# Routed experts on one core: only used rows gathered, results scattered in two column halves, fixed buffers, another general path

## The chip, the cores and the metric

The kernel runs on one core of one Trainium2 chip. What counts is the device time of one execution in microseconds; the median of several runs is given. PE is the matrix engine, PEld its weight loads, DVE, ACT and POOL the vector, scalar and general engines, SP the engine that starts most DMAs.

## The reference, cut to what matters

One layer over 512 tokens of width 1024 in float32: an RMS norm and one wide projection, three attention branches (gated linear attention in chunks, attention over selected keys, attention over a memory of 256 rows), gated output projections, a residual, and then experts in groups:

```
g_sel    = argmax(h @ w_r1 + b_r1)                      # 4 groups
e_prob   = softmax(the 4 logits of that group in h @ w_r2 + b_r2)
top_p, top_i = top_k(e_prob, 2), normed; weight = g_prob * top_p
hid      = silu(h @ w_gate[e]) * (h @ w_up[e]) * weight  # 16 experts, 1024 -> 256
x        = x + sum over e of hid[e] @ w_down[e]          # 256 -> 1024
```

Each token goes to 2 of 16 experts. The kernel returns x, 512 x 1024.

## The kernel before

Products of float32 are made of three passes each (high x high, high x low, low x high): ACT casts a weight tile to its high part (line 94), DVE forms the rest (line 95), PE runs the three products (lines 102 to 104 for the experts). All stages up to the second residual are as in the change and aren't told here. `out_gemm` (line 1016) forms the residual x, POOL multiplies it by the norm's gain (line 1054) and writes it to `h2d` in DRAM (line 1055), ACT's queue writes x itself to `out`. The router (`route`, `place`) finds each token's two experts and its place among an expert's tokens.

An expert has C = 96 slots. `rows` (line 1212) forms `idx0`: for each slot of each expert the token's row. A slot without a token gets a row number from 512 up, and for these `h2d` and `out` have 96 rows more, which a tile of zeros fills (lines 953 to 958).

The loop over the 16 experts (line 1342) runs an order given by letters, `ORDER = "0H12at3bh"`. In round e, "0", "1", "2", "3" are the gate and up products of expert e in four parts (`up`, line 1288; a piece of part 3 takes the raw weight, line 1300), "H" transposes the hidden values of expert e-1, "a" and "b" are the two column halves of its down product (`down`, line 1321), each copied by ACT into half of y (line 1328), "t" transposes the gathered tokens of expert e+1 (`tokens_t`, line 1268), "h" forms the hidden values of e. After "b" the whole y, 96 x 1024, is added to `out` by one indirect DMA of POOL (`scatter`, line 1331). At the start of round e POOL also gathers the tokens of expert e+2 (`gather`, line 1258), and SP fetches the twelve weight tiles of expert e+4 (`fetch`, lines 839 and 844). Expert 0's tokens aren't gathered but placed by products (line 1149).

The gathered tile xg and the result y are taken from one ring of four buffers (`tag="wr"`, `WR = 4`), in the order in which the scheduler reaches them. POOL's DMAs are counted by eight counters, DMASW0 to 7, which they take in turn; SP's and ACT's by DMAHW0 to 7. Each engine runs its instructions in the order laid down at build time.

At the end the largest expert's count is loaded into a register of each engine (line 1378), and a general path runs if it is over 96 (`tc.If`, line 1379): further blocks of 96 slots with gathers and scatters of their own.

```
    got, xt, hid, ht, ys = {}, {}, {}, {}, {}
    got[1] = gather(idx0[:, 1:2])
...
        if e + 2 < ne:
            got[e + 2] = gather(idx0[:, e + 2:e + 3])
...
                    ys[o] = wp.tile([C, D], F32, tag="wr", name="y", bufs=WR)
                else:
                    down(ys[o], *ht[o], wts[o], int(op in "bd"))
                if op in "bd":
                    scatter(ys[o], idx0[:, o:o + 1])
```

Of the kernel before, what the change touches and what calls it, by code (L numbers as in the profile page):

```python
# [18 lines left out]
P = 128  # L19
# [28 lines left out]
def hybrid(ctx, tc, a, out):  # L48
# [904 lines left out]
    zrow = slot([P, 512], F32, "zrow")  # L953
    G.memset(zrow, 0.0)
# [95 lines left out]
    def residual(t, c, ps, x, ss):  # L1050
# [12 lines left out]
        nc.scalar.dma_start(out[t * P:(t + 1) * P, c * 512:(c + 1) * 512], x)  # L1063
# [125 lines left out]
    ne = 16  # L1189

    def mark(c, t0):
# [3 lines left out]
        if c:  # L1195
            p4 = small.tile([P, 4], F32, name="p4")
            V.tensor_scalar(p4, pos[:, tt, :].rearrange("p t c -> p (t c)"), float(-c * C), None, op0=OP.add)
        V.tensor_tensor(out=oh, in0=slots[:, None, :].to_broadcast([P, 4, C]), in1=p4.to_broadcast([P, 4, C]),
                        op=OP.is_equal)
        V.tensor_scalar(vals[:, tt, :, 2], pos[:, tt, :], -1.0, float(c * C - 1), op0=OP.mult, op1=OP.add)  # L1200
        return oh
# [10 lines left out]
    def rows(c, idx):  # L1212
        """c: the chunk of slots; None for the first one, whose marks are kept in ohs0."""
        pi = ap_.tile([C, 16 * 3], F32, tag="lg", name="lg")
        ohs = ohs0 if c is None else []
        for t0, k in ((0, L0), (2, -1)):
            with ExitStack() as held:
                if c is None and k is not None:
                    held.enter_context(tc.issue_after(late[k].ins))
                ohs.append(mark(c or 0, t0))  # L1220
                spread(pi, ohs, 0, 3, t0, False)
# [3 lines left out]
        found = V.tensor_scalar(idx, fi, float(T - 1), None, op0=OP.add)  # L1225
        return found if c is None else ohs
# [9 lines left out]
    # the array stays busy while the last tokens are routed  # L1236
# [12 lines left out]
    found = rows(None, idx0)  # L1249
# [12 lines left out]
    def tokens_t(xg, placed=None):  # L1262
        xH, xL = [], []
        for c in range(2):
            if placed is None:
                tp = ap_.tile([P, 4, C], F32, tag="tp", name="tp")
                for k in range(4):
                    PE.transpose(tp[:, k, :], xg[:, :, 4 * c + k], ident[0:C, 0:C])
            else:
                tp = placed[c]  # L1270
            h = sp.tile([P, 4, C], F32R, tag="x", name="xgh", bufs=4)
            l = sp.tile([P, 4, C], F32R, tag="x", name="xgl", bufs=4)
            raw = sp.tile([P, C], F32, tag="xr", name="xgr", bufs=2) if c else None
            n = 4 - c
            if placed is None:
                split_into(h[:, 0:n, :], l[:, 0:n, :], tp[:, 0:n, :])
            else:
                for k in (0, 2):
                    m = min(k + 2, n)
                    split_into(h[:, k:m, :], l[:, k:m, :], tp[:, k:m, :])  # L1280
# [24 lines left out]
    def hidden(ps, cwt):  # L1305
        hid = half([C, P, 2], F32, "hid")
# [5 lines left out]
    def hidden_t(hid):  # L1312
        tp = ap_.tile([P, 2, C], F32, tag="tp", name="tp")
        for k in range(2):
            PE.transpose(tp[:, k, :], hid[:, :, k], ident[0:C, 0:C])
        hh = half([P, 2, C], F32R, "hh")
        hl = half([P, 2, C], F32R, "hl")
# [3 lines left out]
    def down(y, hh, hl, ws, c):  # L1321
        wh = wp.tile([P, 2, 512], F32R, tag="wh", name="wh", bufs=WH)
        wl = wp.tile([P, 2, 512], F32R, tag="wl", name="wl", bufs=WH)
        ps = gp.tile([C, 512], F32, tag="g", name="g")
# [9 lines left out]
    got, xt, hid, ht, ys = {}, {}, {}, {}, {}  # L1334
    got[1] = gather(idx0[:, 1:2])
# [6 lines left out]
    for e in range(ne):  # L1342
        if e + NF < ne:
            fetch(e + NF, after=found if e == E0 else None)
        if e + 2 < ne:
            got[e + 2] = gather(idx0[:, e + 2:e + 3])
        for op in ORDER if e < ne - 1 else LAST:
# [31 lines left out]
    with tc.If(cval > C):  # L1379
        more = []  # L1380
        for c in range(1, -(-T // C)):
            idx = const.tile([C, ne], I32, name=f"idx{c}")
            cwt = const.tile([C, ne, 2], F32, name=f"cwt{c}")
            ohs = rows(c, idx)
            weights(ohs, cwt)
            more.append((idx, cwt))
        with tc.For_i(0, ne, 1) as e:
            one = bass.ds(e, 1)
            ws = load_expert(*[a[n][one].rearrange("o r c -> (o r) c") for n in ("w_gate", "w_up", "w_down")])
            for idx, cwt in more:  # L1390
                ix = small.tile([C, 1], I32, name="ix")
                V.tensor_copy(ix, idx[:, one])
                cw = small.tile([C, 2], F32, name="cwx")
                V.tensor_copy(cw, cwt[:, one, :].rearrange("p o q -> p (o q)"))
                xH, xL = tokens_t(gather(ix))
                ps = gp.tile([C, 512], F32, tag="g", name="g")
                for kc in range(4):
                    up(ps, xH, xL, ws, kc)
                hh, hl = hidden_t(hidden(ps, cw))
                y = wp.tile([C, D], F32, tag="wr", name="y", bufs=WR)  # L1400
                for i in range(2):
                    down(y, hh, hl, ws, i)
                scatter(y, ix)
# [25 lines left out]
```

## Time and profile before

| | |
|---|---|
| median of 3 runs | 1003.43 us (1003.26 to 1009.3) |
| span of the profiled execution, first to last instruction | 1002.3 us |
| PE busy, share of the span | 943.1 us, 94% |
| DVE, ACT, POOL busy | 639.2, 473.3, 133.0 us |
| DMA | 138.71 MB, 138 GB/s over the span |
| expert loop, first transposes to the last copy into y | 813.4 to 983.8 us |

The page gives one execution; the median of the runs is 1.1 us above its span. Busy shares are means over stages that are bound by different things, so the loop is read stretch by stretch below.

### The profile page before, as it was taken

To read this page: it belongs to the slowest core of one execution; us is meant where nothing else is said; L and a number is where in the kernel's file an instruction comes from. 1 tells how busy PE (TensorE), PEld (TensorE's weight loads), DVE (VectorE), ACT (ScalarE), POOL (GpSimd) and SP (SyncE) were. 2 spreads that over 40 slices of the span, in tenths; PEclk is the share of its full clock that TensorE was granted. 3 is DMA by queue.
4 is the path that set the end of the run, shared out by engine and by line. 5 is a ranking of instruction groups with operands and counts; after the bars stand their busy time and mean duration, and the time that the engine had idled before them with its cause. 6 is when DMAs were issued, how large, how long until landed. Compare 5 with 4: busy or idle time off the path is not lost. (4 is left out here: it accounts for less than half of the span.)

```text
span 1002.3 us, 13004 instructions
## 1 busy us (share of the span) xinstructions
PE 943.1 (94%) x4425; PEld 754.6 (75%) x4425; DVE 639.2 (64%) x1581; ACT 473.3 (47%) x946; POOL 133.0 (13%) x120
## 2 busy tenths in 40 slices
PE   7999999999999969999999999999999889988992
PEld 5778776887888858887888888878888767756661
DVE  6895668779876545467544633662554678867861
ACT  5675443454222524466333323443234258867771
POOL 4002123001320131000000000001011212222221
PEclk9999999999999989999999999999999799999997
DMA  7755221222233212221332222247575379999972
GB/s 230 224 142 158 85 64 43 65 62 83 86 106 90 82 43 66 82 64 43 89 100 85 85 84 85 64 126 252 169 252 177 128 227 324 299 308 313 305 202 46
DMA packets 73529, 138.71 MB, mean 138 GB/s; under 512 B 8930, under 2 KB 11568, under 8 KB 73456
## 3 DMA queue, kind: packets, MB, share of 16 engines
q1 hardware_dynamic: 66656, 119.56, 38.8%
q0 software_dynamic: 5616, 16.14, 7.0%
q10 hardware_dynamic: 1184, 2.11, 0.6%
q8 instruction: 37, 0.61, 0.2%
q14 instruction: 36, 0.29, 0.1%
HBM read 125.59 MB, written 11.27 MB: 137 GB/s over the span
## 5 line engine op out<-in xcount | busy, mean ns | idle before, releaser
L94 ACT CAST wh<-wr 128x1024 fp32r<-128x1024 f32 (+1 forms) x124 | 127.6, 1030 | 263.9 <-PE g L145 154.9
L95 DVE TENSOR_TENSOR wl<-wr,wh 128x1024 fp32r<-128x1024 f32 (+1 forms) x124 | 150.1, 1211 | 151.1 <-ACT wh L94 145.1
L140 PE MATMUL g<-hh,wh 128*128 128x512 f32 (+1 forms) x424 | 169.9, 401 | 0.4 <-DVE mvl L98 0.4
L145 PE MATMUL g<-hl,wh 128*128 128x512 f32 (+1 forms) x424 | 166.7, 393 | 0.0
L146 PE MATMUL g<-hh,wl 128*128 128x512 f32 (+1 forms) x424 | 165.9, 392 | 0.0
L95 DVE TENSOR_TENSOR wl<-mw,wh 128x512 fp32r<-128x512 f32 (+1 forms) x188 | 112.6, 641 | 9.5 <-ACT wh L94 9.4
L94 ACT CAST wh<-mw 128x512 fp32r<-128x512 f32 (+1 forms) x188 | 101.1, 587 | 11.3 <-PE g L104 10.6
L140 PEld LDWEIGHTS g<-hh,wh 128*128 128x128 f32 x424 | 80.8, 191 | 17.8 <-issue 1.9
L146 PEld LDWEIGHTS g<-hh,wl 128*128 128x128 f32 x424 | 80.7, 190 | 16.0
L145 PEld LDWEIGHTS g<-hl,wh 128*128 128x128 f32 x424 | 80.7, 190 | 14.8 <-issue 0.2
L140 PE MATMUL g<-wh,hh 128*128 128x512 f32 x160 | 63.3, 395 | 0.0
L145 PE MATMUL g<-wl,hh 128*128 128x512 f32 x160 | 63.1, 394 | 0.0
L146 PE MATMUL g<-wh,hl 128*128 128x512 f32 x160 | 62.7, 392 | 0.0
L102 PE MATMUL g<-wh,xgh 128*96 128x512 f32 x108 | 48.2, 446 | 0.5 <-ACT wh L94 0.5
L437 POOL PARTITION_ALL_REDUCE dqsq<-dqsq x8 | 26.7, 3359 | 135.2 <-ACT dqsq L429 77.5
L103 PE MATMUL g<-wl,xgh 128*96 128x512 f32 x108 | 43.6, 403 | 0.5 <-DVE wl L95 0.3
L104 PE MATMUL g<-wh,xgl 128*96 128x512 f32 x108 | 43.6, 404 | 0.0
L606 ACT ACTIVATE dp<-dp,nm,rs_y 128x128 f32<-128x128 f32 (+3 forms) x32 | 20.9, 654 | 35.4 <-DVE nm L605 35.3
L964 POOL MEMSET tmp<- 128x128 f32 x1 | 0.2, 205 | 267.6 <-PE tp L795 267.6
L145 PEld LDWEIGHTS g<-wl,hh 128*128 128x128 f32 x160 | 30.2, 189 | 6.2 <-issue 0.5
L140 PEld LDWEIGHTS g<-wh,hh 128*128 128x128 f32 x160 | 30.1, 188 | 6.4 <-issue 0.5
L146 PEld LDWEIGHTS g<-wh,hl 128*128 128x128 f32 x160 | 30.1, 188 | 6.0
(425 smaller groups left out, 2015.7 us busy)
## 6 DMA issues: line engine op xcount, KB each, us to landing
wr<-in_w_in_dram SPq DMA_DIRECT2D x72, 512.0 KB, 3.6
mw<-in_w_gate_dram SPq DMA_DIRECT2D x64, 256.0 KB, 8.1
mw<-in_w_up_dram SPq DMA_DIRECT2D x64, 256.0 KB, 8.2
mw<-in_w_down_dram SPq DMA_DIRECT2D x64, 256.0 KB, 7.8
wr<-in_w_mem_kv_dram SPq DMA_DIRECT2D x16, 512.0 KB, 5.5
wr<-in_w_o_mem_dram SPq DMA_DIRECT2D x8, 512.0 KB, 3.9
wr<-in_w_o_dsa_dram SPq DMA_DIRECT2D x8, 512.0 KB, 3.9
wr<-in_w_o_gla_dram SPq DMA_DIRECT2D x8, 512.0 KB, 3.8
```

The costliest lines, as they stand in the source:

```text
L94: hi = A.copy(h, src)
L95: lo = V.tensor_sub(l, src, h.bitcast(F32))
L102: PE.matmul(ps, sh, mh, start=first, stop=False)
L103: PE.matmul(ps, sh, ml, start=False, stop=False)
L104: PE.matmul(ps, sl, mh, start=False, stop=last)
L140: i = PE.matmul(ps, sh, mh, start=first, stop=False)
L145: PE.matmul(ps, sh, ml, start=False, stop=False)
L146: i = PE.matmul(ps, sl, mh, start=False, stop=last)
L437: G.partition_all_reduce(flat, flat, P, bass_isa.ReduceOp.add)
L606: A.activation(p, p, AF.Exp, bias=nm[:, t:t + 1], scale=rs, accum_out=sm[:, t:t + 1])
L964: G.memset(tmp, 1.0)
```

## The change

The 96 rows of padding in `h2d` and `out` go. Gathers and scatters get a bound: a slot whose row number is over 511 is skipped (`bounds_check=T - 1, oob_is_err=False`). The gathers write into two fixed buffers, cleared once by POOL, so that a skipped slot holds old but finite values; their weights are zero. `out` becomes two tensors, one for each half of the columns. Each half of y is scattered by itself as soon as it is copied, from two fixed buffers in turn. The general path treats all 512 tokens for each expert, with plain DMAs of SP in place of POOL's gathers and scatters. On these inputs the largest expert has 83 tokens, so it isn't entered.

```
-    h2d = tc.dram_tile([T + C, D], F32, name="h2d")
-    for c in range(2):
-        nc.gpsimd.dma_start(h2d[T:T + C, c * 512:(c + 1) * 512], zrow[0:C, :])
-        nc.gpsimd.dma_start(out[T:T + C, c * 512:(c + 1) * 512], zrow[0:C, :])
+    h2d = tc.dram_tile([T, D], F32, name="h2d")
...
-    def gather(idx):
-        xg = wp.tile([C, P, KB], F32, tag="wr", name="xg", bufs=WR)
-        nc.gpsimd.indirect_dma_start(out=xg.rearrange("p i k -> p (i k)"), out_offset=None, in_=h2d[:, :],
-                                     in_offset=bass.IndirectOffsetOnAxis(ap=idx, axis=0))
-        return xg
+    xb = [wp.tile([C, P, KB], F32, tag="wr", name="xg", bufs=WR) for _ in range(2)]
+    yb = [wp.tile([C, 2, 512], F32, tag="wr", name="y", bufs=WR) for _ in range(2)]
+    for x in xb:
+        G.memset(x, 0.0)
+
+    def gather(e):
+
+        nc.gpsimd.indirect_dma_start(out=xb[e % 2].rearrange("p i k -> p (i k)"), out_offset=None, in_=h2d[:, :],
+                                     in_offset=bass.IndirectOffsetOnAxis(ap=idx0[:, e:e + 1], axis=0),
+                                     bounds_check=T - 1, oob_is_err=False)
+        return xb[e % 2]
...
-        A.copy(y[:, c * 512:(c + 1) * 512], ps)
-
-    def scatter(y, idx):
-        nc.gpsimd.indirect_dma_start(out=out, out_offset=bass.IndirectOffsetOnAxis(ap=idx, axis=0),
-                                     in_=y, in_offset=None, compute_op=OP.add)
+        return ps
+
+    def scatter(e, c, ps):
+        y = yb[e % 2][:, c, :]
+        A.copy(y, ps)
+        nc.gpsimd.indirect_dma_start(out=out[c], in_=y, in_offset=None, compute_op=OP.add,
+                                     out_offset=bass.IndirectOffsetOnAxis(ap=idx0[:, e:e + 1], axis=0),
+                                     bounds_check=T - 1, oob_is_err=False)
...
-                    ys[o] = wp.tile([C, D], F32, tag="wr", name="y", bufs=WR)
                 else:
-                    down(ys[o], *ht[o], wts[o], int(op in "bd"))
-                if op in "bd":
-                    scatter(ys[o], idx0[:, o:o + 1])
+                    c = int(op in "bd")
+                    scatter(o, c, down(*ht[o], wts[o], c))
...
             for t in range(NT):
...
+                nc.sync.dma_start(xg.rearrange("p i k -> p (i k)"), h2d[rs, :])
...
+                    nc.sync.dma_start(o, out[c][rs, :])
+                    V.tensor_add(o, o, down(hh, hl, ws, c, P))
+                    nc.sync.dma_start(out[c][rs, :], o)
```

POOL's order in the expert loop, before, from the scatter of expert 0's result on. A row has the line, the tensors (the number tells tiles of one name apart) and what the row waits for:

```order
L1331 DMA out_0_dram<-y_7415,idx0_7150 608x1024 [waits DMAHW5_49,DMAHW3_49,DMAHW6_49,DMAHW1_49,Activation_49]
L1258 DMA xg_7661<-h2d_6440,idx0_7150 96x1024 [waits DMASW3_49]
L1331 DMA out_0_dram<-y_7549,idx0_7150 608x1024 [waits Activation_49]
L1258 DMA xg_7795<-h2d_6440,idx0_7150 96x1024 [waits DMASW5_49,DMASW0_49,PE_49]
L1331 DMA out_0_dram<-y_7683,idx0_7150 608x1024 [waits Activation_49]
L1258 DMA xg_7929<-h2d_6440,idx0_7150 96x1024 [waits DMASW7_49,DMASW1_49,PE_49]
L1331 DMA out_0_dram<-y_7817,idx0_7150 608x1024 [waits Activation_49]
```

And in the changed kernel, from the first half of expert 1's result on:

```order
L1328 DMA out_0_dram<-y_7184,idx0_7144 512x512 [waits DMASW6_49,Activation_49]
L1252 DMA xg_7182<-h2d_6438,idx0_7144 96x1024 [waits DMASW5_49,PE_49]
L1328 DMA out_1_dram<-y_7184,idx0_7144 512x512 [waits DMASW0_49,Activation_49]
L1328 DMA out_0_dram<-y_7183,idx0_7144 512x512 [waits DMASW1_49,Activation_49]
L1252 DMA xg_7181<-h2d_6438,idx0_7144 96x1024 [waits DMASW7_49,PE_49]
L1328 DMA out_1_dram<-y_7183,idx0_7144 512x512 [waits DMASW3_49,Activation_49]
L1328 DMA out_0_dram<-y_7184,idx0_7144 512x512 [waits DMASW4_49,Activation_49]
L1252 DMA xg_7182<-h2d_6438,idx0_7144 96x1024 [waits DMASW2_49,PE_49]
L1328 DMA out_1_dram<-y_7184,idx0_7144 512x512 [waits DMASW6_49,Activation_49]
```

Before, a gather waits for the counter of the scatter in the row above it (the scatters take DMASW3, 5, 7, 1 here), for that of an older gather and for PE, and each scatter for ACT alone. Now a gather waits for the older gather in its buffer and for PE; each half waits for ACT and for the same half of the expert before.

POOL's order around the end of the If, before:

```order
L1387 REGISTER_ALU
L1387 COMPARE_AND_BRANCH
L1387 UNCONDITIONAL_BRANCH [waits DMASW5_49,DMASW4_49,DMASW6_49,DMASW3_49,DMASW7_49,DMASW2_49,DMAHW0_49,DMASW1_49,DMAHW1_49,DMASW0_49,DMAHW2_49,SP_sequencer_49,DMAHW3_49,DVE_sequencer_49,DMAHW4_49,PE_sequencer_49,DMAHW5_49,Activation_se
L1379 ISA [waits DMASW4_49,DMASW5_49,DMASW3_49,DMASW6_49,DMASW2_49,DMASW7_49,DMASW1_49,DMASW0_49]
L1379 UNCONDITIONAL_BRANCH
L1425 ISA [waits barrier_Pool_Activation_PE_DVE_SP_gather]
```

And now:

```order
L1388 REGISTER_ALU
L1388 COMPARE_AND_BRANCH
L1388 UNCONDITIONAL_BRANCH [waits DMASW5_49,DMASW4_49,DMASW6_49,DMASW3_49,DMASW7_49,DMASW2_49,DMAHW0_49,DMASW1_49,DMAHW1_49,DMASW0_49,DMAHW2_49,SP_sequencer_49,DMAHW3_49,DVE_sequencer_49,DMAHW4_49,PE_sequencer_49,DMAHW5_49,Activation_se
L1375 UNCONDITIONAL_BRANCH
L1428 ISA [waits barrier_Pool_Activation_PE_DVE_SP_gather]
```

The ISA row of line 1379, which waits for all eight counters of POOL's DMAs, is gone.

POOL's order where the residual is multiplied, before the loop, first the four zero writes and then the multiplies, before:

```order
L964 MEMSET tmp_6447 128x128 [waits PE_49]
L965 AFFINE_SELECT tmp_6447<-tmp_6447 128x128 [waits Pool_49]
L954 MEMSET zrow_6436 128x512 [waits PE_49]
L957 DMA h2d_6440<-zrow_6436 96x512 [waits DMASW3_49,Pool_49]
L958 DMA out_0_dram<-zrow_6436 96x512
L957 DMA h2d_6440<-zrow_6436 96x512
L958 DMA out_0_dram<-zrow_6436 96x512
L1054 TENSOR_TENSOR xg_6622<-xr_6509,gffn_6420 128x512 [waits DMAHW6_49,DVE_49,Activation_49]
L1055 DMA h2d_6440<-xg_6622 128x512 [waits Pool_49]
```

And now, with the two clears of the fixed buffers:

```order
L1049 TENSOR_TENSOR xg_6616<-xr_6503,gffn_6420 128x512 [waits DMAHW6_49,DVE_49,Activation_49]
L1050 DMA h2d_6438<-xg_6616 128x512 [waits DMASW3_49,Pool_49]
L1248 MEMSET xg_7181 96x1024 [waits DMAHW4_49,DMAHW2_49,DMAHW7_49,DMAHW0_49,Activation_49]
L1049 TENSOR_TENSOR xg_6641<-xr_6505,gffn_6420 128x512 [waits DVE_49]
L1050 DMA h2d_6438<-xg_6641 128x512 [waits Pool_49]
L1049 TENSOR_TENSOR xg_6672<-xr_6507,gffn_6420 128x512 [waits DVE_49]
L1050 DMA h2d_6438<-xg_6672 128x512 [waits Pool_49]
L1049 TENSOR_TENSOR xg_6703<-xr_6509,gffn_6420 128x512 [waits DVE_49]
L1050 DMA h2d_6438<-xg_6703 128x512 [waits Pool_49]
L1248 MEMSET xg_7182 96x1024 [waits DMAHW5_49,DMAHW3_49,DMAHW7_49,DMAHW1_49,DVE_49]
L1049 TENSOR_TENSOR xg_6846<-xr_6727,gffn_6422 128x512 [waits DMAHW7_49,DVE_49,PE_49]
L1049 TENSOR_TENSOR xg_6877<-xr_6729,gffn_6422 128x512 [waits DVE_49,PE_49]
```

The zero writes are gone, and the clears stand after the first and after the fourth multiply. On the other engines the rows up to the If, and their order, are the same as before.

## Rows read from the trace of the kernel before

**Rows 1.** Busy time of each engine in three stretches: the stretch, its length, then busy us (instructions) of PE, PEld, DVE, ACT, POOL, the mean granted PE clock as a share of full speed, the mean busy share of the 16 DMA engines, GB/s.

```profile
813.40:880.00 66.60, 66.60 (x323) 49.12 (x324) 57.17 (x109) 56.08 (x127) 13.34 (x10) 0.97 1.02 311
880.00:966.00 86.00, 75.73 (x345) 54.15 (x344) 62.57 (x116) 61.68 (x135) 17.86 (x14) 0.94 1.04 310
966.00:983.80 17.80, 15.73 (x69) 10.06 (x67) 11.88 (x24) 13.37 (x29) 4.46 (x3) 1.00 0.44 66
```

**Rows 2.** PE's timeline: start, us, engine, line, operation, in brackets the idle time before it and what ended it. L1268 are the transposes of the gathered tokens, L1300 the products with the raw weight.

```profile
813.40 1.25 PE L1268 MATMUL tp<-ident,xg 96*128 96x96 f32 x8 [2.88 <-DMA xg<-h2d,idx]
...
823.50 1.02 PE L1268 MATMUL tp<-ident,xg 96*128 96x96 f32 x8
...
842.65 1.02 PE L1268 MATMUL tp<-ident,xg 96*128 96x96 f32 x8
...
871.51 1.10 PE L1268 MATMUL tp<-ident,xg 96*128 96x96 f32 x8
...
919.03 1.10 PE L1268 MATMUL tp<-ident,xg 96*128 96x96 f32 x8 [2.77 <-DMA xg<-h2d,idx]
...
964.72 1.02 PE L1268 MATMUL tp<-ident,xg 96*128 96x96 f32 x8
...
976.15 1.02 PE L1300 MATMUL g<-mw,xgr 128*96 128x256 f32 x4
```

**Rows 3.** Who waited for whom on PE, 806 to 984 us: us in total, times, longest.

```profile
PE tp L1268 <- DMA xg<-h2d,idx: 13.2, 7, 2.9
```

**Rows 4.** Timeline of POOL, and of ACT's copies into y, columns as in rows 2.

```profile
828.58 1.52 POOL L1331 DMA_INDIRECT out_dram<-y,idx  x1 [12.75 <-ACT y L1328]
...
910.59 1.12 POOL L1258 DMA_INDIRECT xg<-h2d,idx  x1 [9.22 <-PE g L104]
...
910.73 0.59 ACT L1328 COPY y<-g 96x512 f32<-96x512 f32 x1
912.02 1.86 POOL L1331 DMA_INDIRECT out_dram<-y,idx  x1 [0.30 <-ACT wh L94]
...
916.30 0.58 ACT L1328 COPY y<-g 96x512 f32<-96x512 f32 x1 [0.25 <-PE g L104]
...
922.40 0.93 POOL L1258 DMA_INDIRECT xg<-h2d,idx  x1 [8.52 <-PE g L102]
923.63 1.44 POOL L1331 DMA_INDIRECT out_dram<-y,idx  x1 [0.30 <-ACT hid L1308]
```

**Rows 5.** Time from an indirect DMA's start to its landing, us, smallest, median and largest: first all gathers, the first gather alone, then all scatters, and alone those started at 912.02, 923.63 and 988.41.

```profile
DMA to landing us min/median/max: 7.4/8.3/11.2
DMA to landing us min/median/max: 7.4/7.4/7.4
DMA to landing us min/median/max: 5.4/9.5/11.2
DMA to landing us min/median/max: 9.6/9.6/9.6
DMA to landing us min/median/max: 9.3/9.3/9.3
DMA to landing us min/median/max: 5.4/5.4/5.4
```

**Rows 6.** SP's timeline, the starts of weight DMAs: the first of expert 5, of expert 6, and the last of expert 15 (twelve to an expert; x4 is four starts).

```profile
820.97 0.33 SPq L839 DMA_DIRECT2D mw<-in_w_gate_dram  x1
...
830.66 0.33 SPq L839 DMA_DIRECT2D mw<-in_w_gate_dram  x1
...
956.30 0.33 SPq L839 DMA_DIRECT2D mw<-in_w_up_dram  x1
956.98 2.35 SPq L844 DMA_DIRECT2D mw<-in_w_down_dram  x4
```

**Rows 7.** DMA queues from 840 to 960 us: packets, MB, share of 16 engines (q1 is SP's, q0 POOL's); then issues by tensor: count, KB each, median us to landing.

```profile
q1 hardware_dynamic: 16018, 29.17, 74.1%
q0 software_dynamic: 2240, 7.87, 28.6%
...
mw<-in_w_up_dram SPq DMA_DIRECT2D x36, 256.0 KB, 9.0
```

**Rows 8.** The last copies into y on ACT and the last scatter on POOL, columns as in rows 2.

```profile
979.30 0.58 ACT L1328 COPY y<-g 96x512 f32<-96x512 f32 x1
...
982.05 0.58 ACT L1328 COPY y<-g 96x512 f32<-96x512 f32 x1 [1.95 <-PE g L104]
983.18 0.58 ACT L1328 COPY y<-g 96x512 f32<-96x512 f32 x1 [0.55 <-PE g L104]
...
988.41 1.41 POOL L1331 DMA_INDIRECT out_dram<-y,idx  x1 [6.68 <-DMA out_dram<-y,idx]
```

**Rows 9.** SP's waits from 980 to 1003 us: us in total, times, longest.

```profile
SPq L1425 <- DMA out_dram<-y,idx: 12.8, 1, 12.8
SPq L1425 <- PEq L1425: 5.8, 2, 5.2
```

**Rows 10.** POOL's timeline before the loop, columns as in rows 2.

```profile
683.29 0.53 POOL L954 MEMSET zrow<- 128x512 f32 x1 [24.04 <-PE g L145]
...
747.56 1.28 POOL L1054 TENSOR_TENSOR xg<-xr,gffn 128x512 f32<-128x512 f32 x1 [61.21 <-DVE xr L1051]
...
781.46 2.54 POOL L1054 TENSOR_TENSOR xg<-xr,gffn 128x512 f32<-128x512 f32 x2 [20.35 <-PE g L145]
```

More of the change, by code (lines that the diff above doesn't have):

```diff
@@ L1062, in residual @@
         copied.append(A.copy(hT, tp))
-        nc.scalar.dma_start(out[t * P:(t + 1) * P, c * 512:(c + 1) * 512], x)
+        nc.scalar.dma_start(out[c][t * P:(t + 1) * P, :], x)
         yield True
@@ L1189, in hybrid, with mark @@
     ne = 16
-    def mark(c, t0):
+    def mark(t0):
         tt = slice(t0, t0 + 2)
@@ L1210, in spread, with rows @@
                       start=t0 == 0 and k == 0, stop=last and t0 == 2 and k == 3)
-    def rows(c, idx):
+    def rows(idx):
         pi = ap_.tile([C, 16 * 3], F32, tag="lg", name="lg")
-        ohs = ohs0 if c is None else []
         for t0, k in ((0, L0), (2, -1)):
             with ExitStack() as held:
-                if c is None and k is not None:
+                if k is not None:
                     held.enter_context(tc.issue_after(late[k].ins))
-                ohs.append(mark(c or 0, t0))
-                spread(pi, ohs, 0, 3, t0, False)
+                ohs0.append(mark(t0))
+                spread(pi, ohs0, 0, 3, t0, False)
         PE.matmul(pi, ident_b[:, 0:C], padrow.rearrange("p e c -> p (e c)"), start=False, stop=True)
@@ L1248, in hybrid @@
     ohs0 = []
-    found = rows(None, idx0)
+    found = rows(idx0)
     if ahead:
@@ L1278, in tokens_t @@
                 for k in (0, 2):
[L1279 to L1280 removed]
+                    q = min(k + 2, n)
+                    split_into(h[:, k:q, :], l[:, k:q, :], tp[:, k:q, :])
             if c:
@@ L1303, in up, with hidden @@
             mm3(ps, xH[kb], xL[kb], *parts[k], kb == 0, kc == 3)
-    def hidden(ps, cwt):
-        hid = half([C, P, 2], F32, "hid")
+    def hidden(ps, cwt, m=C):
+        hid = half([m, P, 2], F32, "hid")
         hf = hid.rearrange("p i k -> p (i k)")
@@ L1345, in hybrid @@
         if e + 2 < ne:
-            got[e + 2] = gather(idx0[:, e + 2:e + 3])
+            got[e + 2] = gather(e + 2)
         for op in ORDER if e < ne - 1 else LAST:
@@ L1379, in hybrid @@
     with tc.If(cval > C):
[L1380 to L1386, printed above, removed]
+        wk = small.tile([P, NT, 2], F32, name="wk")
+        V.tensor_reduce(wk, vals[:, :, :, 3:6], axis=AX.X, op=OP.add)
+        past = small.tile([P, NT, 2], F32, name="past")
+        V.tensor_scalar(past, pos, float(C), None, op0=OP.is_ge)
+        V.tensor_mul(wk, wk, past)
+        cw = slot([P, NT, 16, 2], F32, "cw")
+        V.tensor_mul(cw[:, :, :, 0], sel[:, :, 0, :], wk[:, :, 0:1].to_broadcast([P, NT, 16]))
+        V.tensor_mul(cw[:, :, :, 1], sel[:, :, 1, :], wk[:, :, 1:2].to_broadcast([P, NT, 16]))
+        V.tensor_add(cw[:, :, :, 0], cw[:, :, :, 0], cw[:, :, :, 1])
+        V.tensor_reduce(cw[:, :, 0, 1], vals[:, :, 0, 6:9], axis=AX.X, op=OP.add)
+        V.tensor_copy(cw[:, :, 1:16, 1], cw[:, :, 0:1, 1].to_broadcast([P, NT, 15]))
         with tc.For_i(0, ne, 1) as e:
@@ L1389, in hybrid @@
             ws = load_expert(*[a[n][one].rearrange("o r c -> (o r) c") for n in ("w_gate", "w_up", "w_down")])
[L1390 to L1396, printed above, removed]
+            for t in range(NT):
+                rs = slice(t * P, (t + 1) * P)
+                cx = small.tile([P, 2], F32, name="cx")
+                V.tensor_copy(cx, cw[:, t, one, :].rearrange("p o q -> p (o q)"))
+                xg = wp.tile([P, P, KB], F32, tag="wr", name="xg", bufs=WR)
+                nc.sync.dma_start(xg.rearrange("p i k -> p (i k)"), h2d[rs, :])
+                xH, xL = tokens_t(xg, m=P)
+                ps = gp.tile([P, 512], F32, tag="g", name="g")
                 for kc in range(4):
                     up(ps, xH, xL, ws, kc)
[L1399 to L1403, printed above, removed]
+                hh, hl = hidden_t(hidden(ps, cx, P), P)
+                for c in range(2):
+                    o = slot([P, 512], F32, "o")
+                    nc.sync.dma_start(o, out[c][rs, :])
+                    V.tensor_add(o, o, down(hh, hl, ws, c, P))
+                    nc.sync.dma_start(out[c][rs, :], o)
 _INS = ["x", "mem", "g_mix", "g_mem", "w_in", "w_gla_a2", "b_gla_a2", "gla_norm", "w_mem_kv",
@@ L1423 @@
                                     kind="ExternalInput").ap()
-    out = nc.dram_tensor("out_0_dram", (T + C, D), F32, kind="ExternalOutput").ap()
+    out = [nc.dram_tensor(f"out_{c}_dram", (T, 512), F32, kind="ExternalOutput").ap() for c in range(2)]
     with tile.TileContext(nc) as tc:
@@ L1427 @@
     r = run_bass_kernel_spmd(nc, [arrays], core_ids=[0])
-    return np.asarray(r.results[0]["out_0_dram"])[:T].reshape(1, T, D)
+    return np.concatenate([np.asarray(r.results[0][f"out_{c}_dram"]) for c in range(2)], axis=1).reshape(1, T, D)
```

40 lines of the change are left out of this document (17 added, 23 removed).

## The prediction

> **What bounds the kernel now.** I read the table of stages first: busy time of each engine in three stretches of the expert loop [rows 1]. The reader is to see three things. From 813.4 to 880 PE has no idle time at all (66.6 of 66.6 us). From 880 to 966 it is idle for 10.3 us, and its mean clock falls from 0.97 to 0.94. And in both stretches the DMA engines are taken up throughout (share 1.02 and 1.04), while DVE and ACT are busy for 86 and 84% of the first stretch and 73 and 72% of the second.
>
> Then I read the starts of the eight transposes with which PE opens the tokens of the next expert, once per expert [rows 2]. I call the one for expert e t(e). From t(2) at 823.50 to t(4) at 842.65 two rounds take 19.15 us, 9.57 each: this is what an expert costs when nobody waits. From t(7) at 871.51 to t(15) at 964.72 it is 93.21 / 8 = 11.65 us. Every late one bears the same mark, a wait for the DMA that writes xg, and the waits of PE in the whole loop are practically that one line: 13.2 us in 7 waits [rows 3]. So the loop is bound by the gathers, not by its arithmetic and not by weights: no cast waits for a weight there.
>
> Why are the gathers late? POOL's timeline shows it [rows 4]. One gather starts at 910.59, the next at 922.40. The scatter between them, started at 912.02, lands after 9.6 us, at 921.6 [rows 5], 0.8 ahead of that second gather. The order of POOL says the same: the gather's row names the completion counter of the scatter above it, because its tile is taken from the ring of four in which that scatter's y lay. The next scatter stands behind that gather in POOL's queue, although its y is complete: y copies end at 910.73 + 0.59 and at 916.30 + 0.58, and the scatter goes at 923.63. The result is a closed ring: gather start 0.93 to 1.12, gap 0.3, scatter landing 9.3 to 9.6 [rows 5], some 0.8 until the next gather, hence 11.3 to 11.8 us per expert whatever the arithmetic needs.
>
> **The change part by part.** Up to the If, the rows of PE, ACT, DVE and SP are the same and in the same order; only POOL's move.
>
> 1. *Fixed buffers.* Gather e+4 now waits for t(e+2), which read its buffer, and for no scatter. The ring is gone. Each gather is started some 18 us before its use and lands after 7.4 to 11.2 [rows 5], so it is late no more. With 9.57 us per expert, t(15) comes at 823.50 + 13 x 9.57 = 947.9 instead of 964.72: **16.8 us**. The wait is replaced by others: scatter (e, c) waits for scatter (e-1, c), one expert earlier, and behind it in POOL's queue stand the gather and the other half. It is late only if a half takes more than 9.57 us to land; a whole one takes 8.8 to 11.2 under load and 5.4 alone [rows 5]. I take 7 to 8 for a half with a third of the bytes. A copy into y waits for the scatter two experts back, which costs nothing at those landings.
>
> 2. *Padding rows.* The reference's router on these inputs gives the experts 45 to 83 tokens, 1024 in all; expert 0 has 78. So the 15 gathers move 946 rows instead of 1440, the scatters 1024 instead of 1536, each now as two rows of 2 KB. What is that worth? SP starts the weights of one expert after another. From 820.97 to 830.66, mostly before the first scatter (828.58 [rows 4]), an expert took 9.69 us; from 830.66 to 959.33 ten took 128.67, that is 12.87 each [rows 6]. So a gather and a scatter cost the weights 3.2 us per expert. The queues agree: 28.6% of 120 us is 34.3 us [rows 7], and 120 us hold 120 / 11.65 = 10.3 pairs: 3.3 us a pair. By bytes a pair shrinks to two thirds: 1.1 us less per expert, 11 us over experts 6 to 15. This decides whether part 1 is paid in full: the last weight that the raw product of expert 15 reads (line 1300) starts at 956.30 and lands 9.0 later, at 965.3 [rows 6, 7]; without stalls PE wants it at 976.15 (that product now [rows 2]) less 16.8 = 959.4, so 6 us must come from here. 11 do. If it were nothing, the weights would hold the end, and part 1 would give 976.15 - 965.3 = 10.8 us. Bounds 10.8 and 18.9 (16.8 and the 2.1 us PE idles after 966 [rows 1]); I take 16.8, by the rows nearest to the changed loop, those of t(2) to t(4).
>
> 3. *The first gather.* t(1) waits 2.9 us for a gather that landed after 7.4 [rows 2, 5]. With 66 rows instead of 96, and one other behind it instead of two, it lands sooner: between 0 and 2.9 us, taken as **1.0**.
>
> 4. *The last scatter.* Now the last copy into y ends at 983.18 + 0.58 = 983.76, the last scatter waits 6.7 us for the one before and starts at 988.41, and lands 5.4 later at 993.8: 10.05 us after the copy [rows 5, 8]. With halves, the one that it waits for starts after the copy of 979.30 + 0.58, 3.9 us before the end, and lands after at most 5.4; POOL is free 1.4 after the copy of 982.05 + 0.58. I take 4.5 for the landing of a half: the last starts 0.9 after the end and lands 5.4 after it. **4.6 us** less; with 5.4 and 3.6 as landings, 3.1 and 6. The Trainium skill (DMA: Bandwidth & Descriptors, Anatomy of one DMA) gives a DMA of POOL some 2.0 us plus bytes at 436 GB/s, by which a whole one would take 2.9 and a half 2.3: the measured 5.4 is nearly twice that, and by the page the split would give 0.6 on the landing where I take 0.9.
>
> 5. *The end of the program.* From the landing at 993.8 to the end of the span at 1002.3 it is 8.5 us, in which SP waits for the last scatter and then 5.2 us more for a barrier [rows 9]. In the order POOL has, on leaving the If, an instruction (ISA) that waits for all eight counters; the changed kernel has no DMA of POOL inside the If and no such row. No row gives its duration. If it was what the barrier waited for, most of the 8.5 can go; if POOL takes as long without it, nothing. Between 0 and 8.5 I take the one wait that a row shows, rounded: **5.0**.
>
> 6. *At no cost.* The two clears of xg (96x1024; the 128x512 one took 0.53, so about 1.1 each) stand among the multiplies of POOL from 747.56 on; the first finds its buffer free, the next multiply after the second comes at 781.46 after 20.35 us of idleness [rows 10]. Without that cover, 2.1 us. The zero rows of h2d and out that go ended long before anyone read them. POOL's 16 further starts (1.4 each, 22 us) fall on an engine that is busy for 17.9 of 86 us [rows 1, 4]. The general path isn't entered (83 tokens at most, 96 slots).
>
> **Sum.** 1002.3 - 16.8 - 1.0 - 4.6 - 5.0 = 974.9 us of span; the median of the runs, 1003.43, is 1.1 above the span of the profiled execution, so **976 us**. With part 5 between 0 and 8.5 and the others near their values, 971 to 983.
>
> **The rivals.**
>
> *The weights hold the end.* Skipped rows may lie on the same few DMA engines, since the used slots of each expert are its first ones; then the fullest engine has as much to do as before, and a weight has landed only when the slowest engine is through. For it: share 1.04 [rows 1], and SP's starts come at the pace of landings. Against it: nothing, as no row tells the engine of a row. Part 1 gives 10.8: 1002.3 - 10.8 - 1.0 - 4.6 - 5.0 + 1.1 = 982; with nothing from part 5, 987.
>
> *The scatters chain themselves.* If a half lands no sooner than the slowest whole one, 11.2 us [rows 5], POOL stalls there instead of at the gather, and the pace stays at 11.2 against 11.65 until the weights are in. Only parts 4 and 5 remain: 1002.3 - 9.6 + 1.1 = 994, no change to speak of.
>
> *Slower: skipped rows still take their turn in POOL's ring.* From the gather start at 922.40 to the landing of the scatter behind it, at 923.63 + 9.3 = 932.9, 192 rows take 10.5 us, some 8.5 of it without the start, 44 ns a row. The change has 3 x 96 = 288 row places per expert. If each takes its turn whatever it holds, that is 12.7 us per expert; from 265 places on it is slower than 11.65. With 12.7 for the 11 experts until the weights are in and 9.6 for the other four, the last scatter starts at 828.6 + 139.7 + 38.4 = 1006.7, lands 5.4 later, and the run ends near 1006.7 + 5.4 + 3.5 + 1.1 = 1017. Against it: if only the 191 used rows count it is 8.4, below 9.57. The Trainium skill (DMA: Bandwidth & Descriptors, Queues, rings and completion order) has each DMA engine go round its queues packet by packet, which makes turns and not bytes the price; by that rule even the used rows, 191 against 192, would give part 2 nothing, which is the first rival.
>
> **How the numbers follow.** Forecast 0.60, weights 0.22, chained scatters 0.08, skipped rows in the ring 0.06; 0.04 for less than 968. The range reaches from 968 over the first rival to 991 and leaves out about 0.18. Two runs of this kernel can be told apart from about 1%, 10 us: faster by more than that (below 993.4) are the forecast, the first rival and the 0.04, 0.86; within it the second, 0.08; slower the third, 0.06.
>
> **What would show it.** Right: t(e) to t(e+1) near 9.6 us up to t(15), no wait of PE for xg after the first, PE's share above 95% from 880 on; SP's weight starts 11 to 12 us apart per expert and over by 950; POOL's scatters in halves without waiting for their own predecessors; last landing some 5 us after the last copy, and 2 to 4 us from there to the end. Wrong: PE waiting for a cast of a weight near t(14) (first rival), POOL waiting 8 us or more at line 1328 for a DMA on out (second), landings of halves above 10 us (third), or starts of indirect DMAs much longer than 1.4 us.

## The result, and the profile after

The changed kernel takes 973.68 us (median of 4 runs, 971.8 to 976.18) beside 1003.35 for the kernel before in the same comparison: ratio 0.9719, 95% interval 0.9684 to 0.9753. A second comparison, on another occasion, gave 975.41 and 0.9757 (0.9728 to 0.9785). The forecast was 976. The profiled execution spans 974.5 us, where the sum said 974.9. (The profile of the first run of fixed buffers alone shows an execution of 1145 us at a mean granted clock of 0.77 and isn't read.)

The stretches of the loop after, columns as in [rows 1]:

```profile
812.00:880.00 68.00, 67.92 (x331) 50.46 (x332) 58.57 (x111) 57.14 (x129) 24.67 (x19) 0.97 1.02 319
880.00:947.00 67.00, 67.00 (x331) 49.70 (x331) 60.02 (x113) 59.24 (x134) 26.45 (x20) 1.00 1.01 314
947.00:963.90 16.90, 15.88 (x77) 11.09 (x75) 12.38 (x25) 13.25 (x29) 6.58 (x5) 1.00 0.52 131
```

PE has no idle time from 880 to 947, and the clock is full there, against 10.3 idle us and 0.94 before [rows 1]. Its waits in the loop, as in [rows 3], are now two:

```profile
PE tp L1263 <- DMA xg<-h2d,idx: 2.9, 1, 2.9
PE g L102 <- ACT hh L94: 0.4, 1, 0.4
```

The timeline after, columns as in [rows 2, 4, 6]: PE's t(1), t(2) and t(15), a triple of POOL's starts in the loop, SP's first weight start of expert 6 and last of expert 15, ACT's last copies into y and POOL's last starts.

```profile
812.08 1.40 PE L1263 MATMUL tp<-ident,xg 96*128 96x96 f32 x8 [2.89 <-DMA xg<-h2d,idx]
...
822.12 1.02 PE L1263 MATMUL tp<-ident,xg 96*128 96x96 f32 x8
...
826.45 0.42 SPq L839 DMA_DIRECT2D mw<-in_w_gate_dram  x1
...
918.99 1.41 POOL L1328 DMA_INDIRECT out_dram<-y,idx  x1 [3.91 <-ACT y L1327]
920.70 1.11 POOL L1252 DMA_INDIRECT xg<-h2d,idx  x1 [0.31 <-PE g L104]
923.01 1.42 POOL L1328 DMA_INDIRECT out_dram<-y,idx  x1 [1.20 <-ACT y L1327]
...
945.40 2.45 SPq L844 DMA_DIRECT2D mw<-in_w_down_dram  x4
...
946.67 1.02 PE L1263 MATMUL tp<-ident,xg 96*128 96x96 f32 x8
...
963.03 1.40 POOL L1328 DMA_INDIRECT out_dram<-y,idx  x1 [1.28 <-ACT y L1327]
963.33 0.58 ACT L1327 COPY y<-g 96x512 f32<-96x512 f32 x1 [0.58 <-PE g L104]
965.46 1.40 POOL L1328 DMA_INDIRECT out_dram<-y,idx  x1 [1.03 <-DMA out_dram<-y,idx]
```

From t(2) to t(15) it is 124.55 / 13 = 9.58 us an expert: the pace without waits, to the end. A half is scattered as soon as ACT has copied it, and the gather that stood closed in the ring [rows 4] goes 0.3 us after a scatter's start has ended. POOL, busy 17.9 of 86 us before [rows 1], is now busy 26.5 of 67, and PE has no idle time there.

Where the time went is seen best when each profile is cut at five marks, all read from timelines like this one (span 1002.3 before, 974.5 after): t(1), t(15), the end of the last copy into y, the end of POOL's last start, the end of the span. The column in brackets is a part of the one before it: the loop from t(2) on. The pieces of all kernels, in us:

| kernel | t(1) at | t(1) to t(15) | (t(2) to t(15)) | to the last copy's end | to the end of POOL's last start | to the end |
|---|---|---|---|---|---|---|
| before | 813.40 | 151.32 | (141.22) | 19.04 | 6.06 | 12.48 |
| changed | 812.08 | 134.59 | (124.55) | 17.24 | 2.95 | 7.64 |
| changed, second time | 808.31 | 133.07 | (124.55) | 17.20 | 2.95 | 7.57 |
| before, fixed buffers | 810.08 | 137.43 | (127.65) | 17.86 | 5.46 | 12.27 |
| before, rows skipped | 812.78 | 145.79 | (135.74) | 18.38 | 4.29 | 12.66 |
| before, both | 812.16 | 137.02 | (125.93) | 17.81 | 4.54 | 12.87 |
| before, no POOL DMA in the If | 812.45 | 148.47 | (138.40) | 19.83 | 4.99 | 7.66 |
| changed, POOL DMA in the If | 810.81 | 134.69 | (124.59) | 18.92 | 2.89 | 12.19 |
| changed, rows moved again | 811.13 | 135.35 | (125.34) | 17.81 | 3.14 | 7.97 |
| changed, scattered whole | 807.50 | 138.12 | (129.61) | 18.18 | 4.50 | 7.60 |
| changed, every row skipped | 812.02 | 133.07 | (124.55) | 17.20 | 2.26 | 7.65 |
| changed, slots spread | 811.22 | 134.64 | (124.56) | 17.23 | 2.34 | 7.67 |
| before, rows skipped and slots spread | 811.15 | 144.59 | (134.45) | 17.19 | 4.47 | 12.00 |

t(1) differs by up to 5.9 us between kernels that are nearly alike up to there, and by 3.8 between two profiles of the changed one. A difference of medians of some 4 us between two of these kernels therefore proves nothing by itself. The first round isn't a fair piece either: t(1) to t(2) takes 8.52 us in the second profile of the changed kernel, where the mean granted clock was 1.00 in it, 10.04 in the first, where it was 0.83, and 11.09 in "before, both", where it was 0.73. From t(2) on the two profiles of the changed kernel agree to 0.01 us, so loops are compared there. Even so it is one profile of each kernel: the kernel before and the one without POOL's DMAs in the If have the same loop, and it takes 141.22 in one and 138.40 in the other.

### The profile page after: what moved, and what is told of

It is laid out like the page before. It is cut to its first block, busy times and chain, and to the rows that moved or that the text cites. A ratio compares the mean times of both kernels' runs of the same rounds, so it can differ in the third digit from the quotient of the medians.

```text
span 974.5 us, 13092 instructions
## 1 busy us (share of the span) xinstructions
PE 935.2 (96%) x4425; PEld 751.9 (77%) x4425; DVE 639.0 (66%) x1581; ACT 472.1 (48%) x946; POOL 153.5 (16%) x133
## 4 chain that ended last, share of the span: by engine, by line
PE 82%; DVE 7%; issue 3%; DMA 3%; ACT 2%; POOL 2%; SPq 0%; POOLq 0%; DVEq 0%; ACTq 0%
PE g L140 18%; PE g L145 18%; PE g L146 18%; PE g L104 4%; PE g L103 4%; PE g L102 4%; DVE wl L95 2%; PE g L1295 1%; PE tp L1263 1%; DMA hx<-in_x_dram 1%; PE g L1144 1%; ACT wh L94 1%; PE lg L1067 1%; DMA xg<-h2d,idx 1%; PE tp L623 1%
## 5 line engine op out<-in xcount | busy, mean ns | idle before, releaser
L1328 POOL DMA_INDIRECT out_dram<-y,idx x32 | 45.5, 1422 | 89.8 <-ACT y L1327 83.1
L437 POOL PARTITION_ALL_REDUCE dqsq<-dqsq x8 | 26.5, 3330 | 134.7 <-ACT dqsq L429 76.9
```

Of the source, the lines that this page charges most:

```text
L437: G.partition_all_reduce(flat, flat, P, bass_isa.ReduceOp.add)
L1328: nc.gpsimd.indirect_dma_start(out=out[c], in_=y, in_offset=None, compute_op=OP.add, out_offset=bass.IndirectOffsetOnAxis(ap=idx0[:, e:e + ...
```

## The experiments

**Fixed buffers alone**, on the kernel before (rows moved, whole scatters, old general path), run twice:

```
+    xb = [wp.tile([C, P, KB], F32, tag="wr", name="xg", bufs=WR) for _ in range(2)]
+    yb = [wp.tile([C, D], F32, tag="wr", name="y", bufs=WR) for _ in range(2)]
...
-            got[e + 2] = gather(idx0[:, e + 2:e + 3])
+            got[e + 2] = gather(idx0[:, e + 2:e + 3], xb[e % 2])
...
-                    ys[o] = wp.tile([C, D], F32, tag="wr", name="y", bufs=WR)
+                    ys[o] = yb[o % 2]
```

> The kernel before with one part of the change: gathers and results in two fixed buffers each; padding rows moved, results scattered whole, general path as before. My theory (the ring is gone, but the weights then hold the end, and whole scatters, each of which waits for the one before, follow at their landing of 9.5 plus 0.8): t(e) 9.6 us apart at first, later held up by weights or by y; weight starts 12 to 13 us per expert as before; last landing 986 to 990 instead of 993.8; 993 to 999 us. Rival 'the buffers alone give the gain': t(15) at 947, 985 to 986 us. Rival 'buffers are nothing': 1003.

Measured 987.43, ratio 0.9862 (0.9836 to 0.9887): below my 993 and near the rival. Once more:

> The kernel before with fixed buffers alone once more, for a profile at the ordinary clock. Time 987 again. Theory (fixed buffers end the waits for gathers; the rest of the distance to the changed kernel is the end: POOL's last start and what follows it): t(15) at 947 to 950, PE waits for no gather after the first; 12.5 us from the end of POOL's last start to the end of the span instead of 7.6. Rival (weights hold it back): t(15) at 953, casts wait for weights for more than 5 us in all.

985.34, ratio 0.9856 (0.982 to 0.9891). PE's t(14) and t(15) and the longest wait between, and who waited in the loop (us in total, times, longest):

```profile
935.25 1.02 PE L1272 MATMUL tp<-ident,xg 96*128 96x96 f32 x8
...
940.66 0.48 PE L102 MATMUL g<-wh,xgh 128*96 128x512 f32 x1 [1.45 <-ACT wh L94]
...
947.51 0.69 PE L1272 MATMUL tp<-ident,xg 96*128 96x96 f32 x5
```

```profile
ACT wh L94 <- DMA mw<-in_w_gate_dram: 3.5, 2, 2.8
PE tp L1272 <- DMA xg<-h2d,idx: 3.2, 1, 3.2
PE g L102 <- ACT wh L94: 1.4, 1, 1.4
ACT wh L94 <- DMA mw<-in_w_up_dram: 1.4, 3, 0.8
```

No gather is late after the first. The buffers alone take 13.6 us out of t(2) to t(15) (141.22 to 127.65; 10.8 against the 138.40). The last round is 12.26 instead of 9.58 because casts wait for weights, and the round before it 10.14: the weights hold the end of the loop, as in the first rival, and take back 3.1 us of it (127.65 against 124.55 in the changed kernel), not 6.

**Skipped rows alone**, on the kernel before:

```
+                                     bounds_check=T - 1, oob_is_err=False)
```
(in `gather` and in `scatter`)

> The kernel before with the other part alone: slots without a token are skipped in gathers and scatters of the loop (and no more), the ring of four buffers, whole scatters and the general path as before. My theory (a scatter's landing time goes by its bytes): landing under load falls from 9.5 to about 6.4, so the ring of 1.0 + 0.3 + landing + 0.8 falls to 8.5 us, under the 9.57 of the arithmetic, and the ring stops binding though it is still there: t(15) near 947 to 950, 978 to 983 us. Rival 'landing is set by the rows' turns or by the weights in the queues': landing stays 9 or more, rounds 11 to 12, 999 to 1003 us. If landing is 8, rounds of 10.1, about 987.

998.24, ratio 0.9975 (0.9952 to 0.9997), where I had 978 to 983. My theory fell. POOL in the loop, and PE's waits:

```profile
907.68 1.80 POOL L1332 DMA_INDIRECT out_dram<-y,idx  x1 [0.30 <-ACT wh L94]
917.36 1.33 POOL L1258 DMA_INDIRECT xg<-h2d,idx  x1 [7.89 <-PE g L103]
919.00 1.80 POOL L1332 DMA_INDIRECT out_dram<-y,idx  x1 [0.31 <-ACT wh L94]
928.99 0.98 POOL L1258 DMA_INDIRECT xg<-h2d,idx  x1 [8.18 <-PE g L103]
```

```profile
PE tp L1269 <- DMA xg<-h2d,idx: 10.9, 7, 2.7
```

Gather to gather is 11.63 us here. With a third of the rows gone the scatters from 823 to 955 us still land after a median of 9.2 us, against 9.6 before in the same stretch. The ring stays closed.

**Both**, on the kernel before:

> The kernel before with fixed buffers and skipped rows together; scatters whole and the general path as before. My theory: t(15) at 947 as in the changed kernel; the end as before (8.5 us behind the last landing) and a whole scatter last: 977 to 982 us. Against the run with skipped rows alone it shows what the buffers are worth once the rows are skipped: nothing if the landing fell under 7.3, several us if not.

984.95, ratio 0.984 (0.9806 to 0.9875): above my 977 to 982, as casts wait for weights in the last round here too (11.09 us), although a third of the rows is skipped. From t(2) to the last copy it is 1.8 us shorter than fixed buffers alone (125.93 + 17.81 against 127.65 + 17.86), and the medians agree within their intervals.

**Rows moved again**, on the changed kernel (zeroed padding rows, no bounds):

```
-    h2d = tc.dram_tile([T, D], F32, name="h2d")
+    h2d = tc.dram_tile([T + C, D], F32, name="h2d")
...
-                                     bounds_check=T - 1, oob_is_err=False)
+                                     )
```

> The changed kernel with its padding rows moved again (96 rows more in h2d and in both halves of out, filled with zeros; no bounds): 288 rows per expert through POOL's queue instead of 192. Forecast's own case (weights hold the end): t(15) some 6 us later than in the changed kernel, PE waits for weights from about e = 12 on, landings of halves up to 6; 981 to 987 us. Rival 'each row takes its turn whatever its size' (44 ns a row place, 12.7 us per expert): 1010 to 1017 us. Rival 'only the buffers matter': 974 to 976.

977.38, ratio 0.9766 (0.9742 to 0.9791), where my own case had 981 to 987; behind t(1) 1.9 us more than the changed kernel over all four pieces. 288 rows per expert take no 12.7 us: rounds are 9.58 but for the last, 10.38, in which casts wait 2.1 us for weights, and the halves of 96 rows land after a median of 7.5 us, at most 8.3. The third rival is out.

**Whole scatters**, on the changed kernel (`out` is one tensor again):

```
...
-        y = yb[e % 2][:, c, :]
-        A.copy(y, ps)
+        A.copy(yb[e % 2][:, c, :], ps)
+        if c == 0:
+            return
+        y = yb[e % 2].rearrange("p c k -> p (c k)")
...
```

> The changed kernel with results scattered whole: both halves copied into y, then one indirect DMA of 4 KB rows into one out tensor. My theory: nothing in the loop (t(15) at 947, PE without waits); at the end one whole scatter behind the last copy instead of half of one: its landing 5 instead of 4.5, its start later where the scatter of expert 14 is late. 974 to 977 us. Rival 'halves are what keeps the loop going': scatters chain themselves at more than 9.6 us each, t(15) later, over 980.

978.38, ratio 0.9771 (0.9751 to 0.9792), where I had 974 to 977 and nothing lost in the loop. It reached t(1) 4.6 us earlier than the changed kernel's first profile, ran at 9.58, and lost 5.1 us in the last two rounds, 13.92 and 10.29, in which ACT's casts wait for weights:

```profile
ACT wh L94 <- DMA mw<-in_w_gate_dram: 4.9, 4, 2.7
ACT wh L94 <- DMA mw<-in_w_up_dram: 2.5, 4, 1.0
```

The changed kernel's second profile reached t(1) 0.8 us later than this one, yet lost nothing. The scatters don't chain themselves in either, so the second rival is out. At the end POOL's last start comes 1.55 us later than with halves, and the rest is the same 7.60 us.

**The end**, from both sides: the kernel before without POOL's DMAs in the general path, and the changed kernel with one kind of them put back:

```
-                xH, xL = tokens_t(gather(ix))
+                xg = wp.tile([C, P, KB], F32, tag="wr", name="xg", bufs=WR)
+                nc.sync.dma_start(xg.rearrange("p i k -> p (i k)"), h2d[0:C, :])
+                xH, xL = tokens_t(xg)
...
-                scatter(y, ix)
+                nc.sync.dma_start(out[0:C, :], y)
```

> The kernel before; only inside the general path, which isn't entered, POOL's gathers and scatters are replaced by plain DMAs of SP (as the path stands it would compute something else there). So POOL issues no DMA inside the If, and the instruction that waits for all eight counters at the end of the If goes. My theory (that instruction and what follows it hold the barrier): 4 to 5 us less between the last landing and the end, 4.6 instead of 8.5, 998 to 1000 us. Rival 'POOL takes as long without it, and the shorter end came from the smaller scatter': 1003, end 8.5.

```
-                    nc.sync.dma_start(o, out[c][rs, :])
+                    nc.gpsimd.dma_start(o, out[c][rs, :])
```

> The changed kernel; inside the general path, which isn't entered, the loads of out go by POOL's queue instead of SP's. My theory: the instruction at the end of the If comes back, 3.9 us more between the last landing and the end: 977 to 978.5 us, end 8.5. Rival 'the end got shorter for another reason': 973.7, end 4.6.

996.8, ratio 0.9959 (0.994 to 0.9979), and 980.54, ratio 0.9787 (0.976 to 0.9814): 1.2 below my range and 2.0 above it. The second one's profile has 1.7 us more up to the last copy than the changed kernel (18.92 against 17.24), in which casts wait 2.1 us for weights. POOL's last start and the span in the first:

```profile
core 0 of [0], span 993.4 us
...
984.33 1.41 POOL L1331 DMA_INDIRECT out_dram<-y,idx  x1 [5.38 <-DMA out_dram<-y,idx]
```

and in the second:

```profile
core 0 of [0], span 979.5 us
...
965.90 1.41 POOL L1328 DMA_INDIRECT out_dram<-y,idx  x1 [0.93 <-DMA out_dram<-y,idx]
```

993.4 - 985.74 = 7.66 and 979.5 - 967.31 = 12.19. The table shows it throughout: 12.0 to 12.9 us with such a DMA, 7.6 to 8.0 without, though the If is never entered. That the ISA row is what takes the time isn't shown, as no row gives its duration.

**No rows at all**, on the changed kernel (nothing of the experts is added to `out`):

```
-        return V.tensor_scalar(idx, fi, float(T - 1), None, op0=OP.add)
+        return V.tensor_scalar(idx, fi, float(3 * T), None, op0=OP.add)
```

> The changed kernel with all row numbers of the slots moved beyond the bound, so that every row of every gather and scatter is skipped; no routed result is added to out. My theory (a skipped row costs next to nothing, and gathers and scatters cost the weights 2.3 to 3.3 us per expert): weight starts 9.6 to 9.9 us per expert, set by the buffers and PE; t(e) 9.58 apart as before; last landing 2 us sooner: 969 to 972 us. Rival 'skipped rows take their turn': weight starts stay at 12 us per expert.

973.05, where I had 969 to 972. DMA queues from 835 to 910 us (packets, MB, share of 16 engines):

```profile
q1 hardware_dynamic: 14091, 25.66, 99.4%
q0 software_dynamic: 2688, 0.02, 2.0%
```

2688 packets take 2% of 75 us on 16 engines, 9 ns each. They belong to 24 DMAs of 96 rows; if all that time were the rows', it would be 10.4 ns a row. So a skipped row costs next to nothing. The weights of experts 6 to 15 are started from 825.83 to 916.36, 9.05 us per expert against 12.14 in the changed kernel (826.45 to 947.85). And the piece behind POOL's last start is 7.65 us although that start moved no row. SP's longest wait behind the last landing, columns as in [rows 9], first in the changed kernel, then with no rows:

```profile
SPq L1428 <- PEq L1428: 4.1, 2, 3.6
SPq L1428 <- PEq L1428: 5.7, 2, 5.1
```

An earlier landing is made up for by a longer wait: what ends the program isn't the last landing.

**The same rows, other slots.** The used slots of an expert are its first ones. If neighbouring rows go to the same engine, for instance in blocks of six, the skipped ones all lie on a few engines. On the changed kernel:

```
-        G.iota(slots, pattern=[[1, C]], base=0, ...
+        G.iota(slots, pattern=[[1, 16], [16, 6]], base=0, ...
...
-        V.tensor_copy(padrow[:, :, 2], pcol.to_broadcast([P, 16]))
+        V.memset(padrow[:, :, 2], 1.0)
...
-        V.tensor_scalar(vals[:, tt, :, 2], pos[:, tt, :], -1.0, -1.0, ...
+        V.tensor_scalar(vals[:, tt, :, 2], pos[:, tt, :], 0.0, -1.0, ...
```

> The changed kernel with the slots of an expert in another order: tokens take slots 0, 6, 12, ..., 90, then 1, 7, ... instead of 0, 1, 2, .... The same rows move and the same rows are skipped. Theory A (rows are dealt to the DMA engines in blocks of six, so the skipped ones, the last slots, all lie on the last few engines and the fullest engine has as much to do as before): the skipped third is now saved on every engine; SP's queue moves 28.5 MB or more from 835 to 940 us instead of 27.35, the weights of experts 6 to 15 are started in 112 to 117 us instead of 120.8 to 124.3. The time hardly moves, since PE holds the loop: 970 to 973. Theory B (the rows are spread anyway, and a landing is long for another reason): both as in the changed kernel, 120 to 124 us, 27 MB.

And the same on the kernel before with skipped rows:

> The kernel before with skipped rows (ring of four, whole scatters, general path as before) and the slots in the order 0, 6, 12, ...: the run with skipped rows alone plus that one thing. Theory A (blocks of six): every engine has four rows instead of six, a scatter's landing under load falls from about 9 to 6.5, the ring to 8.6 us, under the 9.57 of the arithmetic: PE waits for no gather, t(15) near 947 to 951, 980 to 985 us. Theory B: as without the spread, 995 to 999, and PE waits for six or more gathers.

Beside them the changed kernel again:

> The changed kernel itself once more, beside the other three on one chip, to compare them with: 972 to 975, ratio 0.972.

975.0, ratio 0.9752 (0.9721 to 0.9782), where I had 970 to 973; 987.66, ratio 0.9884 (0.9852 to 0.9916), between the ranges of both theories; 975.41. The queues from 835 to 910 us in the changed kernel:

```profile
q1 hardware_dynamic: 10702, 19.49, 76.9%
q0 software_dynamic: 2651, 4.16, 24.4%
```

and with its slots spread, with SP's first weight start of expert 6 and last of expert 15:

```profile
q1 hardware_dynamic: 11510, 20.96, 80.6%
q0 software_dynamic: 2685, 4.21, 25.4%
```

```profile
824.32 0.33 SPq L839 DMA_DIRECT2D mw<-in_w_gate_dram  x1
...
932.23 4.04 SPq L844 DMA_DIRECT2D mw<-in_w_down_dram  x4
```

POOL moves the same bytes, yet the weights flow 7.5% faster and ten experts are started in 111.95 us instead of 121.4. So the outcome of theory A holds for the weights. The two shares add to 106.0% spread and to 101.3% unspread; with all rows moved they add to 70.4 + 35.7 = 106.1%. That fits engines that idled, unspread, while the fullest held up each weight. The Trainium skill (DMA: Bandwidth & Descriptors, Why a DMA increments its semaphore by 16 and not by 1) has a tile of 96 partitions dealt over all 16 engines; by an estimate from it that makes six rows each. No row here names an engine, so the dealing is inferred from the two streams, and other ways of keeping neighbouring rows together would fit as well. The time doesn't move, as PE holds the loop.

For landings theory A fell: with rows skipped and spread, PE still waits for gathers (8.2 us in 6 waits), and whole scatters land after a median of 8.9. Still the ratio is 0.9884 against 0.9975 without the spread, some 9 us. The two profiles lie 4.5 us apart (989.4 and 993.9), 1.3 of it from t(2) to t(15); where the rest comes from they don't show.

## Why the prediction was right, step by step

*Fixed buffers, 16.8.* Right, and the main cause: 151.32 - 134.59 = 16.7 us behind t(1), all of it from t(2) on, and fixed buffers alone give 13.6 of it on the kernel before. What bound that loop was the ring of landings, as [rows 2 to 4] were read. The last round gave 1.8 us more (19.04 to 17.24), the bound that I had not taken.

*Padding rows, decisive for 6 us.* Here a step failed, in two ways that cancelled. I put the stream's gain at 1.1 us per expert by bytes. With rows moved again the weights of experts 6 to 15 took 125.4 us (825.37 to 950.76). With them skipped they took 121.4 and 122.8 in the two profiles of the changed kernel, and 125.1 in the one with POOL's DMA back in the If: between nothing and 0.4 per expert. The cause that fits is the first rival's, that the skipped rows lay on a few engines; spread, the gain is 1.35. And I held the landing of the last weights at 965.3 unless rows were saved. But in the kernel with rows moved again SP's last weight start ends at 950.76, 8.6 us earlier than before [rows 6], of which 5.3 lie in an earlier start of expert 6's. How much of that is the earlier t(1) of those executions and how much buffers that come free sooner isn't settled. So weights without the skip cost 0.8 us in the loop with halves (125.34 against 124.55 from t(2) on), where I had 6. With whole scatters the weights hold the last rounds with the skip as well: 3.1 us lost without it, 1.4 and 5.1 with it (127.65, 125.93 and 129.61). I had put the halves at nothing in the loop; in these profiles only kernels with halves ran to t(15) without losing anything to the weights. Why the weights keep up better beside halves isn't shown.

The third rival's remark that turns and not bytes are the price isn't borne out. From 835 to 910 us POOL's queue took 35.2% of the engines for 6.27 MB in 1786 packets (fixed buffers, whole rows) and 35.7% for 6.29 MB in 2687 packets (rows moved again, halves), but 2.0% for 2688 packets of skipped rows.

*First gather, 1.0.* Wrong. PE waits 2.89 us for it as before (2.88 [rows 2]), with 66 rows or 96 (3.08 with rows moved again). t(1) came 1.3 us earlier, but that is less than two executions of one kernel differ. With every row skipped the wait is 1.4.

*Last scatter, 4.6.* Too large: 6.06 - 2.95 = 3.1 us, which is the earlier start. That start waits for the scatter before it to land. From the chain that ended last, start, us from start to landing: in the kernel before, in the one with whole scatters and skipped rows, in the changed one, and with no rows:

```profile
980.32 7.33 DMA out_dram<-y,idx
960.19 5.94 DMA out_dram<-y,idx
960.26 4.43 DMA out_dram<-y,idx
958.68 2.61 DMA out_dram<-y,idx
```

So a half does land in about the 4.5 that I took, and that is why POOL's last start comes 1.55 us sooner than with whole scatters. But the landing of the last one, which I priced at 0.9, isn't on the path: the piece behind its start is 7.64 with halves and 7.60 with whole rows. By an estimate from the Trainium skill (DMA: Bandwidth & Descriptors, Anatomy of one DMA) a half with skipped rows would land 0.6 us sooner than a whole with all of them. Here the difference is 7.33 - 4.43 = 2.9, and still 1.6 against the 6.03 of the kernel before without POOL's DMAs in the If.

*End of the program, 5.0.* Right in size, 4.8 us (12.48 to 7.64), and that POOL's DMAs in the If cause it is shown from both sides: 4.8 us less without them, 4.55 more with one put back. Read from the last landing, as I did [rows 9], the piece was badly cut, since its length is the same from POOL's last start and not from the landing.

*At no cost.* POOL's tile rows show the clears at their hidden place, 0.96 us each:

```profile
L1248 POOL MEMSET xg<- x2: 944/958/971, 748.6 to 760.1; 96x1024 f32 x2
```

They weren't tried by themselves.

The sum: 16.7 + 1.8 + 1.3 + 3.1 + 4.8 = 27.7, to the rounding the 27.8 between the spans, where I had 27.4. That it agrees within 0.4 us is partly luck: the 1.8 that I had left out and the 1.3 of the earlier t(1) stand for the 2.5 that the last scatter and the first gather lacked, and t(1) alone differs by 3.8 between two profiles of one kernel.

## What to carry to other kernels

Look for a tile that takes its buffer in turn with tiles of another kind: a load that waits for a store's landing closes a ring that sets the pace whatever its engines do, and two fixed buffers for each kind open it. Which rows are skipped mattered more to the other stream than how many: the same third gave it at most 0.4 us per expert in one place and 1.35 spread out, so try both. Cut profiles at marks in the program and compare the pieces, here from the second round on: whole times of one kernel differ by more than most of these edits are worth.

## What the runs showed of the hardware

A DMA of POOL in a branch that is never taken cost 4.55 and 4.8 us at the end of the program in the two pairs that test it: 12.0 to 12.9 us behind POOL's last start instead of 7.6 to 8.0, in every profile in the table. What POOL does in the 7.6 that remain is open; no row names it.

A skipped row of an indirect DMA costs about 9 ns of one DMA engine, counted by packets (2688 packets, 2.0% of 16 engines for 75 us).

A landing beside the stream of weights hardly follows the rows. With the ring, whole scatters of 96 rows land after a median of 9.6 us, with a third of them skipped 9.2, with those spread 8.9. With fixed buffers it is 8.6, with a third skipped 8.5, and halves of 96 rows take 7.5. Behind the last weights it does follow them: 7.33, 5.94, 4.43 and 2.61 us in the rows above. What a landing is made of while the weights fill the queues stays open.
